# Layer 1's output projection as seven half-size products, with positions as rows

## The chip, the cores and the metric

The kernel runs on one core of one Trainium2 chip. The metric is the time of one execution on the device, in microseconds (us). The kernel before takes 930.77 us, the median of 3 runs (930.66 to 931.35).

## The reference, cut to what matters

Two layers work on x, 512 positions by 1024 features: an mLSTM mixer, then a gated linear attention (GLA) mixer. Each ends with an output projection, an RMSNorm over the features and a residual. What the change touches is the end of layer 1:

```python
def gla_mixer(h, w_in, w_gate_up, b_gate, norm_w, w_out):
    ...
    on = o * lax.rsqrt(jnp.mean(o * o, axis=-1, keepdims=True) + NORM_EPS)
    y = on.reshape(B, T, D_INNER) * _f32(norm_w) * jax.nn.silu(z)
    return jnp.einsum('bte,ed->btd', y, _f32(w_out))
...
    x = x + rms_norm(out, post_norm_w[i]).astype(x.dtype)
```

y is 512 x 2048, w_out is 2048 x 1024.

## The kernel before, in words

Everything is float32 in and out. To multiply at the fast format of TensorE (PE), each operand is split into a high part (a cast on ScalarE, ACT, L133) and a low part (a subtraction on VectorE, DVE, L134), and a product is three matmuls: high x high, high x low, low x high.

Activations lie with features on the partitions and positions in the free axis. The program is a list of jobs in the order of PE (`job`, `run_jobs`, from L137). A job that needs weights names a chunk, 128 x 1024; chunks are loaded by SyncE's queue (SP) into three buffers (`raw`), split into four pairs (`whi`, `wlo`), and are split LA = 3 chunks ahead of the job that runs. PE, ACT and DVE keep the order of the program; GpSimd (POOL) and SP are ordered by the scheduler. `later(k, fn)` puts off work on other engines by k jobs, `steps` spreads it over jobs.

Layer 1's head h has four jobs `gv`, attention (`g_att`, L1071), four jobs `gz`, and `g_y` (L1082), which multiplies y's blocks by their norm and splits them (`y_split`). The output projection (`out_stage(1, ...)`, L1120) then takes the weights as stationary operand and y as moving operand, half of the sequence at a time, 256 columns: 16 blocks of y's features x 8 blocks of output x 2 halves x 3 = 768 matmuls. A chunk serves 24 or 48 of them. The sum of squares over features crosses partitions, so it goes through PE as well (`rstd_of`, `ssq`). `residual` (L769) reads layer 0's result x1 back from memory (stored by `x1_done`, L829), scales and adds. The output is written transposed, features by positions, and the host turns it.

The lines that matter in the stage:

```python
            proj(ps, chunk, yhi[r], ylo[r], c == 0, c == 1, sl)
            if c == 1:
                ...
                nc.scalar.mul(pair(OUT["o", half, n // 2])[:, n % 2, :], ps, col(PV_POST + KD * layer + n))
```

Of the kernel before, what the change touches and what calls it, by code (L numbers as in the profile page):

```python
# [16 lines left out]
P = 128  # L17
# [5 lines left out]
NH = 4  # L23
# [69 lines left out]
def tile_mlstm_gla(ctx, tc, xT, pvec, cst, wg, wgv, w_min, w_qk, w_v, w_mout,  # L93
                   w_gqk, w_gr, w_gu, w_gv, w_gz, w_gout, lvl_masks, outT):
# [22 lines left out]
    def mm(out, lhsT, rhs, start, stop):  # L117
        nc.tensor.matmul(out, lhsT=lhsT, rhs=rhs, start=start, stop=stop)  # L118
# [51 lines left out]
    def run_jobs():  # L170
        srcs = [x for j in jobs for x in j[1]]
        raws, ready, used = [], [], 0
        for fn, ss, n, b, la in jobs:
            used += len(ss)
            while len(ready) < min(used + la, len(srcs)):
                while len(raws) < min(len(ready) + 3, len(srcs)):
                    raws.append(load_raw(srcs[len(raws)][0]))
                i = len(ready)
                ready.append(split_chunk(raws[i], srcs[i][1]))
# [6 lines left out]
            for _ in range(n):  # L186
# [9 lines left out]
    ring = lambda ap: (ap, "ring")  # L196
    keep = lambda ap: (ap, "keep")

# [82 lines left out]
    # The first projections take x * w; their rstd follows when it is known.  # L281
# [46 lines left out]
    # the part of the gates that comes from v, by products with rows of weights  # L328
# [200 lines left out]
    # gates: rows (head, block) of log i and log f, their decays and running maximum  # L529
# [206 lines left out]
    def out_full(layer, n, mid=None):  # L736
        """Rows 128 n of out^T from the first half of its inputs, for all of the sequence."""
# [7 lines left out]
        job(run, ring((w_mout, w_gout)[layer][2 * n]))  # L745

    def out_job(layer, n, c, half, after=None):
        """A half of the sequence of rows 128 n of out^T, from the half c of its inputs."""
        sl = HALF[half]

        def run(chunk):
# [17 lines left out]
        job(run, ring((w_mout, w_gout)[layer][2 * n + c]))  # L769

    def residual(half, src, done, last=False):
        """Steps of out = x + rms_norm(out), in place, for a half of the sequence."""
# [14 lines left out]
        def add(k):  # L787
# [3 lines left out]
            if k > 1:  # L791
                done(k - 2, pair(o(k - 2)), half)
            if 1 <= k <= KP:
                eng = nc.gpsimd if last and k == 2 else nc.vector
                eng.tensor_add(o(k - 1), o(k - 1), xr[k - 1])  # L795
# [4 lines left out]
    def out_stage(layer, early, after_half, done=0, ahead=0):  # L800
        for n in range(done, NF):
            out_full(layer, n, early if n == done and not layer else None)
            if n == done and layer:
                job(early, n=0)
        for n in range(NF, NF + ahead):
            out_job(layer, n, 0, 0)
        for half in range(2):
            for n in range(KD):
                if n >= NF + ahead * (half == 0):
                    out_job(layer, n, 0, half)  # L810
                out_job(layer, n, 1, half, after_half if (n, half) == (0, 1) else None)

    for h in range(NH):
        job(lambda h=h: (m_num(h), m_scale(h), m_skip(h)), n=0)
        if h < NH - 1:
# [16 lines left out]
    def x1_done(kp, x1, half):  # L832
# [12 lines left out]
        nc.sync.dma_start(x1_d[half, kp], x1)  # L845

    def after_half0():
        rstd, add = residual(0, x_rows, x1_done)
# [10 lines left out]
    # projections take x1 * w; their rstd follows  # L859
# [120 lines left out]
    def kept_a(w, j, kind, la=LA):  # L980
# [4 lines left out]
        job(run, (w_gqk[w, j], kind), n=2, la=la)  # L985
# [97 lines left out]
    def g_y(h, vt):  # L1083
# [46 lines left out]
    def early1():  # L1130
        g_rstd(NH - 1)
        steps.extend([lambda v=v: (g_y(NH - 1, v), g_y(NH - 1, v + 1)) for v in (0, 2)])

    def x_done(k, x, half):
        nc.sync.dma_start(outT[2 * k * P:2 * (k + 1) * P, HALF[half]].rearrange("(a p) t -> p a t", p=P), x)

    x1_rows = lambda k, half: pair(x1_d[half, k])

    def after_half1():
        rstd, add = residual(0, x1_rows, x_done)  # L1140
        steps.append(rstd)
        for k in range(KP + 2):
            steps.extend([lambda k=k: add(k), lambda: None])
# [7 lines left out]
def _host(inputs):  # L1151
# [46 lines left out]
    out["w_gout"] = outc(a["g_w_out"].reshape(E, D))  # L1198
    lm = np.zeros((8, P, P), np.int32)
    for i, half in enumerate([64, 32, 16, 8, 4, 2, 1]):  # L1200
# [7 lines left out]
        "w_gqk", "w_gr", "w_gu", "w_gv", "w_gz", "w_gout", "lvl_masks"]  # L1208
# [18 lines left out]
```

## Time and profile before

| | |
|---|---|
| median of 3 runs | 930.77 us (930.66 to 931.35) |
| span of the profiled execution, first to last instruction | 928.9 us |
| the profiled execution's own time | not listed apart; the median lies 1.9 us above its span |
| PE busy | 916.0 us, 99% |
| DVE busy | 617.2 us, 66% |
| ACT busy | 516.4 us, 56% |
| POOL busy | 150.8 us, 16% |
| mean granted clock of TensorE | 0.997 |
| bytes moved | 114.06 MB, mean 123 GB/s |

Busy time is the time in which an engine had an instruction under way; PE's matmuls overlap, so a busy PE is not a PE at its peak. Idle time of an engine matters where another one waits for it. The stage that the change replaces begins at 824.1 us and ends with the span.

### The profile page before, as it was taken

The page shows a single profiled execution, that of the slowest core. Times are in us where ns is not written, and L with a number is a line of the kernel's source. Part 1 is how long each engine was busy: PE and PEld are TensorE (multiplying, and loading weights), DVE is VectorE, ACT ScalarE, POOL GpSimd, SP SyncE. Part 2 cuts the span into 40 slices and gives each one's busy share as a digit, 9 for nine tenths or more (in the row PEclk, how much of TensorE's full clock was granted, in tenths as well). Part 3 has the DMA queues.
Part 4 walks back from the last instruction along what each step waited for, and adds up shares of the span by engine and source line. Part 5 has one row for each costly group of instructions (what it writes and reads, how often), then busy time and mean ns, then how long its engine had stood idle before and what let it go on. Part 6 is the DMA issues. An engine that isn't in the chain of part 4 may idle for free. (4 is left out here: it accounts for less than half of the span.)

```text
span 928.9 us, 13051 instructions
## 1 busy us (share of the span) xinstructions
PE 916.0 (99%) x5030; PEld 787.8 (85%) x5030; DVE 617.2 (66%) x863; ACT 516.4 (56%) x855; POOL 150.8 (16%) x111
## 2 busy tenths in 40 slices
PE   9999999999999999999999999999999999999995
PEld 6887878878877888899999987778888888899995
DVE  5999897787795668787668666642446454565563
ACT  6856676655754657775666454553335353545451
POOL 0022563163240045233002100000000000000000
PEclk9999999999999999999999999999999999999998
DMA  8334353442431323332777322122312222124573
GB/s 313 118 111 147 114 167 128 134 150 91 146 126 46 93 66 114 114 114 94 219 247 237 133 72 87 68 69 93 91 68 73 87 91 91 58 62 152 184 227 114
DMA packets 41669, 114.06 MB, mean 123 GB/s; under 512 B 4545, under 2 KB 9025, under 8 KB 41601
## 3 DMA queue, kind: packets, MB, share of 16 engines
q1 hardware_dynamic: 41312, 112.95, 37.6%
q8 instruction: 41, 0.67, 0.3%
q14 instruction: 28, 0.22, 0.1%
q10 hardware_dynamic: 288, 0.22, 0.1%
HBM read 104.76 MB, written 8.39 MB: 122 GB/s over the span
## 5 line engine op out<-in xcount | busy, mean ns | idle before, releaser
L134 DVE TENSOR_TENSOR wlo<-raw,whi 128x1024 fp32r<-128x1024 f32 (+1 forms) x159 | 202.8, 1280 | 138.3 <-ACT whi L133 137.4
L133 ACT CAST whi<-raw 128x1024 fp32r<-128x1024 f32 (+1 forms) x159 | 164.2, 1037 | 99.2 <-PE gv L118 37.7
L118 PE MATMUL op<-yhi,whi 128*128 128x256 f32 x512 | 146.5, 286 | 0.0
L118 PE MATMUL op<-yhi,wlo 128*128 128x256 f32 x512 | 144.9, 283 | 0.4 <-DVE wlo L134 0.4
L118 PE MATMUL op<-ylo,whi 128*128 128x256 f32 x512 | 145.3, 284 | 0.0
L341 POOL TENSOR_TENSOR vp<-V,wv 128x512 f32<-128x512 f32 x56 | 88.5, 1603 | 177.3 <-ACT V L429 109.1
L118 PEld LDWEIGHTS op<-ylo,whi 128*128 128x128 f32 x512 | 98.2, 192 | 1.3 <-issue 0.7
L118 PEld LDWEIGHTS op<-yhi,whi 128*128 128x128 f32 x512 | 98.2, 192 | 0.8 <-issue 0.7
L118 PEld LDWEIGHTS op<-yhi,wlo 128*128 128x128 f32 x512 | 98.2, 192 | 0.6 <-DVE wlo L134 0.6
L344 DVE SCALAR_TENSOR_TENSOR vp<-V,wv 128x512 f32<-128x512 f32 x72 | 68.0, 985 | 0.0
L118 PE MATMUL gz<-g2h,whi 128*128 128x512 f32 x128 | 51.6, 403 | 0.3 <-PEq L1067 0.3
L118 PE MATMUL gz<-g2h,wlo 128*128 128x512 f32 x128 | 49.9, 390 | 0.0
L118 PE MATMUL gz<-g2l,whi 128*128 128x512 f32 x128 | 49.9, 389 | 0.0
L118 PE MATMUL qk<-chi,whi 128*128 128x512 f32 x128 | 49.8, 389 | 0.0
L118 PE MATMUL qk<-chi,wlo 128*128 128x512 f32 x128 | 49.8, 389 | 0.0
L118 PE MATMUL qk<-clo,whi 128*128 128x512 f32 x128 | 49.8, 389 | 0.0
L118 PE MATMUL gv<-whi,g2h 128*128 128x512 f32 x128 | 49.8, 389 | 0.0
L118 PE MATMUL gv<-wlo,g2h 128*128 128x512 f32 x128 | 49.8, 389 | 0.0
L118 PE MATMUL gv<-whi,g2l 128*128 128x512 f32 x128 | 49.8, 389 | 0.0
L795 POOL TENSOR_TENSOR o<-o,xr 128x512 f32<-128x512 f32 x1 | 1.5, 1491 | 293.6 <-DVE o L790 293.6
L118 PE MATMUL z<-hhi,whi 128*128 128x512 f32 x112 | 44.2, 394 | 0.0
L118 PE MATMUL z<-hlo,whi 128*128 128x512 f32 x112 | 43.6, 390 | 0.0
(240 smaller groups left out, 2219.5 us busy)
## 6 DMA issues: line engine op xcount, KB each, us to landing
raw<-in_w_min SPq DMA_DIRECT2D x30, 512.0 KB, 3.7
raw<-in_w_mout SPq DMA_DIRECT2D x29, 512.0 KB, 4.2
raw<-in_w_gout SPq DMA_DIRECT2D x29, 512.0 KB, 3.5
wv<-in_wgv SPq DMA_DIRECT2D x32, 256.0 KB, 3.5
raw<-in_w_qk SPq DMA_DIRECT2D x16, 512.0 KB, 3.5
raw<-in_w_gqk SPq DMA_DIRECT2D x16, 512.0 KB, 3.7
raw<-in_w_gz SPq DMA_DIRECT2D x16, 512.0 KB, 3.4
raw<-in_w_gv SPq DMA_DIRECT2D x16, 512.0 KB, 3.5
```

Source lines behind the costliest of these rows:

```text
L118: nc.tensor.matmul(out, lhsT=lhsT, rhs=rhs, start=start, stop=stop)
L133: nc.scalar.copy(hi, src)
L134: nc.vector.tensor_sub(lo, src, hi.bitcast(F32))
L341: nc.gpsimd.tensor_mul(j, V[h][i], w)
L344: nc.vector.scalar_tensor_tensor(j, V[h][i], 1.0, w, op0=ALU.mult, op1=ALU.mult, accum_out=o)
L795: eng.tensor_add(o(k - 1), o(k - 1), xr[k - 1])
```

## The change

The two products of 2 x 2 blocks (y: halves of the positions by halves of its 2048 features; weights: halves of the features by halves of the outputs) are made by seven products of blocks instead of eight. y's block is now the stationary operand (128 positions at a time), the weights move, 512 wide, and positions are the output's rows. Each product is 4 chunks x 2 blocks of 128 positions x 2 feature blocks x 3 = 48 matmuls of 512 columns. P1 to P7 name the products; a job takes one chunk c of one, 12 matmuls: P1 0, P5 0, P1 1, P5 1, and so on, then P2, P3, P6, P7 mixed, and P4 at the end, 24 matmuls for each block of positions.

The sums and differences of weight blocks are formed chunk by chunk on POOL (`p5`, `p2`, `p7`, 16 instructions of 128 x 1024), those of y's blocks on POOL for k below 4 and for heads 0 and 1, and on DVE for the others (`combine`). y's blocks and their combinations are split as operands 1 to 4. With positions as rows, the norm's sum is taken by ACT along the free axis, and the post-norm weight, now along the free axis, comes as a row (`pw`). x1 is therefore needed with positions as rows: `turn` transposes it on PE in layer 0's output stage, 4 transposes for each of 8 tiles. A chunk may have its own buffers (`home`, tiles of the pool t5), is formed up to FLA chunks before it is split and loaded up to HLA chunks ahead. The output is written as it is wanted.

```diff
+FLA = 2
+HLA = 3
+NRAW = 3
...
-        job(run, ring((w_mout, w_gout)[layer][2 * n + c]))
+        job(run, ring(w_mout[2 * n + c]))
...
-        nc.sync.dma_start(x1_d[half, kp], x1)
+        x1 = pair(x1)
+
+        def turn():
+            ps, xn = psum("xt"), t2("xn")
+            for j in range(2):
+                for i in range(2):
+                    nc.tensor.transpose(ps[:, (2 * j + i) * P:(2 * j + i + 1) * P],
+                                        x1[:, i, j * P:(j + 1) * P], ident)
+            nc.scalar.copy(xn, ps)
+            nc.sync.dma_start(x1_d[2 * half:2 * half + 2, :, kp * 256:(kp + 1) * 256].rearrange("j p c -> p j c"),
+                              xn.rearrange("p (j c) -> p j c", j=2))
+
+        later(8 if half == 0 else 4, turn)
...
         nc.vector.tensor_mul(y, y, st["rs", h])
-        if vt:
-            y_split(h, [vt - 1])
-        if vt == 3:
-            y_split(h, [3])
+        if h < 2:
+            Y[0, n] = y
+            nc.gpsimd.tensor_sub(y[:, HALF[1]], y[:, HALF[1]], y[:, HALF[0]])
+        else:
+            Y[1, n - 8] = y
...
+        if h == NH - 1:
+            job(lambda: [operand("2", k, Y[1, k]) for k in range(4)], n=0)
+            job(lambda: [combine(k, nc.gpsimd) for k in range(4)], n=0)
         job(lambda h=h: g_att(h))
...
+                if h == 2:
+                    job(lambda i=i: [operand("1", k, Y[0, k]) for k in range((0, 2, 5)[i - 1], (2, 5, 8)[i - 1])], n=0)
...
+    def operand(name, k, src):
+
+        OPS[name, k] = t2("yhi", F32R), t2("ylo", F32R)
+        split(*OPS[name, k], src)
+
+    def combine(k, eng):
+
+        y1, y2 = Y[0, k], Y[1, k]
+        a, b = HALF
+        eng.tensor_sub(y1[:, b], y2[:, b], y1[:, b])
+        eng.tensor_sub(y1[:, a], y1[:, b], y1[:, a])
+        eng.tensor_sub(y2[:, a], y2[:, a], y1[:, b])
...
+    def p5(c):
+        def f(a21, a22):
+            nc.gpsimd.tensor_add(a21, a21, a22)
+            sm[c] = a21
+            return a21
+
+        def to_s2():
+            sub(sm[c], sm[c], raw11[c])
+
+        return source([(w_gout[1, 0, c], lambda: t5("sm")[:, 0:1024]), (w_gout[1, 1, c], None)], form=f,
+                      after=to_s2, free=(1, 0))
...
+        def to_s4():
+            sub(raw12[c], raw12[c], sm[c])
...
+    def p7(c):
+        def f(a22):
+            sub(sm[c], a22, sm[c])
+            raw22[c] = a22
+            return sm[c]
+
+        def to_p4():
+            last[c] = split_chunk(raw22[c], "t2")
...
+    for c in range(4):
+        prod_job("P1", c)
+        prod_job("P5", c)
+        if c == 1:
+            job(lambda: (g_rstd(NH - 1), steps.extend(
+                [lambda: tail_y(0), lambda: tail_y(2), lambda: None, lambda: None]
+                + [lambda k=k: (combine(k, nc.vector), combine(k + 1, nc.vector)) for k in (4, 6)]
+                + [lambda k=k: (operand("3", k, Y[0, k]), operand("3", k + 1, Y[0, k + 1])) for k in range(0, 8, 2)]
+                + [lambda c=c: operand4(c) for c in range(4)])), n=0)
...
+    for name, c in (("P2", 0), ("P2", 1), ("P3", 0), ("P2", 2), ("P3", 1), ("P2", 3), ("P3", 2),
+                    ("P6", 0), ("P6", 1), ("P6", 2), ("P6", 3), ("P3", 3), ("P7", 0), ("P7", 1), ("P7", 2)):
+        prod_job(name, c)
+    job(lambda: [load_res(r) for r in (2, 3)], n=0)
+    prod_job("P7", 3)
+    job(lambda: [load_res(r) for r in (0, 1)], n=0)
+
+    def last_row(r):
+        part_sum(r, 1, bank["a", r])
+        part_scale(r, 1, bank["a", r], nc.vector)
+        row_done(r)
+
+    job(lambda: product("P4", "a", last, 0), n=2)
+    job(lambda: (product("P4", "a", last, 1), last_row(0), last_row(1)), n=13)
```

How the change moves instructions is shown at three places. First DVE, from the last head's gz jobs to the evacuation of its attention (`g_att(3)`); pt are y's blocks, ylo their low parts, wlo a chunk's low part. Before:

```order
L1097 TENSOR_TENSOR gz_8444<-gz,rs_238 128x512
L1086 TENSOR_TENSOR pt_8225<-pt_8225,rs 128x512
L134 TENSOR_TENSOR ylo_8449<-pt_8224,yhi_8448 128x512
L1086 TENSOR_TENSOR pt_8226<-pt_8226,rs 128x512
L134 TENSOR_TENSOR ylo_8454<-pt_8225,yhi_8453 128x512
L134 TENSOR_TENSOR ylo_8458<-pt_8226,yhi_8457 128x512
L1079 SCALAR_TENSOR_TENSOR pt_8461<-o,pv,gz_8325 128x512
```

And now:

```order
L1144 TENSOR_TENSOR gz_8505<-gz,rs_238 128x512
L1132 TENSOR_TENSOR pt_8263<-pt_8263,rs_8369 128x512
L1132 TENSOR_TENSOR pt_8264<-pt_8264,rs_8369 128x512
L138 TENSOR_TENSOR ylo_8511<-pt1_7892,yhi_8510 128x512
L138 TENSOR_TENSOR ylo_8515<-pt2_7893,yhi_8514 128x512
L138 TENSOR_TENSOR ylo_8519<-pt3_7894,yhi_8518 128x512
L138 TENSOR_TENSOR ylo_8523<-pt0_8261,yhi_8522 128x512
L138 TENSOR_TENSOR ylo_8527<-pt1_8262,yhi_8526 128x512
L138 TENSOR_TENSOR ylo_8531<-pt2_8263,yhi_8530 128x512
L138 TENSOR_TENSOR ylo_8535<-pt3_8264,yhi_8534 128x512
L1125 SCALAR_TENSOR_TENSOR pt0_8550<-o_8554,pv_80,gz12_8364 128x512
```

Seven ylo splits stand between the last gz and the first product of g_att(3), where three stood.

Second POOL, around the stage's start; sm and raw are weight chunks, a is the chunk of P1, pt are y's blocks. Before, POOL's list from layer 1's scores to the end is:

```order
L975 AFFINE_SELECT GA_6132<-GA_6132 128x128 x4
L1066 TENSOR_LOAD wide
L1067 COMPARE_AND_BRANCH
L1067 UNCONDITIONAL_BRANCH x2
L795 TENSOR_TENSOR o<-o,xr 128x512
L1223 UNCONDITIONAL_BRANCH
```

Now, from the first weight sum on:

```order
L1241 TENSOR_TENSOR sm<-sm,raw 128x1024 x2
L1200 TENSOR_TENSOR pt_7525<-pt_8261,pt_7525 128x256
L1201 TENSOR_TENSOR pt_7525<-pt_7525 128x256
L1246 TENSOR_TENSOR sm<-sm,a_8183 128x1024
L1200 TENSOR_TENSOR pt_7526<-pt_8262,pt_7526 128x256
L1201 TENSOR_TENSOR pt_7526<-pt_7526 128x256
L1241 TENSOR_TENSOR sm<-sm,raw 128x1024
```

After these come nine more instructions on y's blocks and twelve more on weight chunks of 128 x 1024, then six that scale parts of the output.

Third DVE within the stage, before, where a chunk's split and a sum of squares alternate:

```order
L134 TENSOR_TENSOR wlo<-raw,whi 128x1024 x2
L257 TENSOR_TENSOR sq<-sq 128x256
L134 TENSOR_TENSOR wlo<-raw,whi 128x1024 x2
L257 TENSOR_TENSOR sq<-sq 128x256
L134 TENSOR_TENSOR wlo<-raw,whi 128x1024
```

And now, from P2 2's split on (L1200 to L1202 are `combine`):

```order
L1200 TENSOR_TENSOR pt_7893<-pt_8552,pt_7893 128x256
L1201 TENSOR_TENSOR pt_7893<-pt_7893 128x256
L1202 TENSOR_TENSOR pt_8552<-pt_8552,pt_7893 128x256
L1200 TENSOR_TENSOR pt_7894<-pt_8553,pt_7894 128x256
L1201 TENSOR_TENSOR pt_7894<-pt_7894 128x256
L1202 TENSOR_TENSOR pt_8553<-pt_8553,pt_7894 128x256
L138 TENSOR_TENSOR wlo<-raw,whi 128x1024
L138 TENSOR_TENSOR ylo<-pt_7525,yhi 128x512
L138 TENSOR_TENSOR ylo<-pt_7526,yhi 128x512
L138 TENSOR_TENSOR wlo<-raw,whi 128x1024
```

Between two splits there now stand six combinations or two splits of y's blocks, and a chunk is 12 matmuls, not 24 or 48.

## Rows read from the trace of the kernel before

**Rows 1.** Page, part 1: busy us (share of the span) xinstructions.

```profile
PE 916.0 (99%) x5030; PEld 787.8 (85%) x5030; DVE 617.2 (66%) x863; ACT 516.4 (56%) x855; POOL 150.8 (16%) x111
```

**Rows 2.** Chain of waits in order of time: start us, us, what.

```profile
764.40 21.76 PE gv L118 x96
...
824.10 5.80 PE op L118 x48
829.90 0.86 PE ssq L118 x2
830.76 51.82 PE op L118 x432
882.58 0.43 PE ssq L118 x2
883.01 34.54 PE op L118 x288
917.55 0.43 PE ssq L118 x2
...
918.03 0.71 PE ssq L118 x2
```

**Rows 3.** Tile rc (ns min/median/max, starts), and PE's timeline at 536.5 us.

```profile
L915 PE MATMUL rc<-cs,rs x4: 271/272/273, 536.6 to 536.9; 128*128 128x128 f32 x4
...
536.55 0.60 PE L915 MATMUL rc<-cs,rs 128*128 128x128 f32 x4
```

**Rows 4.** Timelines of POOL and DVE, 921 us on: start, us, what [idle before].

```profile
921.25 1.49 POOL L795 TENSOR_TENSOR o<-o,xr 128x512 f32<-128x512 f32 x1 [293.60 <-DVE o L790]
...
923.81 1.28 DVE L795 TENSOR_TENSOR o<-o,xr 128x512 f32<-128x512 f32 x2
```

**Rows 5.** Groups by form, whole run (first two), 824 on (last): busy, mean ns | idle.

```profile
L133 ACT CAST whi<-raw 128x1024 fp32r<-128x1024 f32 x155 | 161.8, 1048 | 97.9 <-PE gv L118 37.7 <-PE gqk L118 29.2 <-PE op L118 13.7
...
L257 DVE TENSOR_TENSOR sq<-sq 128x256 f32<-128x256 f32 x27 | 11.3, 420 | 10.4 <-ACT sq L254 10.4
...
L134 DVE TENSOR_TENSOR wlo<-raw,whi 128x1024 fp32r<-128x1024 f32 x26 | 31.9, 1225 | 28.2 <-ACT whi L133 28.2
```

**Rows 6.** DVE's timeline at 837 us, POOL at rest.

```profile
837.50 1.23 DVE L134 TENSOR_TENSOR wlo<-raw,whi 128x1024 fp32r<-128x1024 f32 x1 [1.18 <-ACT whi L133]
838.65 0.68 DVE L1086 TENSOR_TENSOR pt<-pt,rs 128x512 f32<-128x512 f32 x1
839.25 0.68 DVE L134 TENSOR_TENSOR ylo<-pt,yhi 128x512 fp32r<-128x512 f32 x1
```

**Rows 7.** DVE's timeline at 126 and 228 us, POOL at work throughout.

```profile
126.13 1.28 DVE L134 TENSOR_TENSOR qkl<-qk,qkh 128x512 fp32r<-128x512 f32 x2
...
228.68 1.78 DVE L344 SCALAR_TENSOR_TENSOR vp<-V,wv 128x512 f32<-128x512 f32 x1
...
230.39 1.76 DVE L344 SCALAR_TENSOR_TENSOR vp<-V,wv 128x512 f32<-128x512 f32 x1
...
232.08 2.30 DVE L134 TENSOR_TENSOR wlo<-raw,whi 128x1024 fp32r<-128x1024 f32 x1
234.31 1.78 DVE L344 SCALAR_TENSOR_TENSOR vp<-V,wv 128x512 f32<-128x512 f32 x1
```

**Rows 8.** POOL's timeline at 327 us, one instruction with gaps on both sides.

```profile
327.17 1.29 POOL L646 TENSOR_TENSOR sq<-sq 128x512 f32<-128x512 f32 x1 [60.78 <-ACT sq L644]
```

**Rows 9.** Timelines of DVE and ACT around the end of g_att(3).

```profile
821.01 1.40 DVE L1079 SCALAR_TENSOR_TENSOR pt<-o,pv,gz 128x512 f32<-128x512 f32 x2
...
826.99 1.04 ACT L133 CAST whi<-raw 128x1024 fp32r<-128x1024 f32 x1
...
828.05 1.23 DVE L134 TENSOR_TENSOR wlo<-raw,whi 128x1024 fp32r<-128x1024 f32 x1 [0.24 <-ACT whi L133]
```

**Rows 10.** Page, part 6: DMA issues, KB each, median us to landing.

```profile
raw<-in_w_gout SPq DMA_DIRECT2D x29, 512.0 KB, 3.5
```

**Rows 11.** Windows: PE, PEld, DVE, ACT, POOL busy, PEclk, DMA share, GB/s.

```profile
923.00:924.00 1.00, 0.00 (x0) 0.00 (x0) 1.00 (x3) 0.00 (x0) 0.00 (x0) 0.65 0.66 222
```

More of the change, by code (lines that the diff above doesn't have):

```diff
@@ L115, in psum, with mm @@
         return pp.tile([P, T], F32, tag="ps", bufs=8, name=name)
-    def mm(out, lhsT, rhs, start, stop):
-        nc.tensor.matmul(out, lhsT=lhsT, rhs=rhs, start=start, stop=stop)
+    def mm(out, lhsT, rhs, start, stop, more=False):
+        nc.tensor.matmul(out, lhsT=lhsT, rhs=rhs, start=start, stop=stop, skip_group_check=more)
     HALF = [slice(0, T // 2), slice(T // 2, T)]
@@ L185, in run_jobs @@
                 x[1]()
-            for _ in range(n):
+            for _ in range(steps_n):
                 if steps:
@@ L194, in run_jobs, with source @@
         jobs.clear()
-    ring = lambda ap: (ap, "ring")
-    keep = lambda ap: (ap, "keep")
+    def source(loads, kind="ring", form=None, after=None, free=(0, 1)):
+        return dict(loads=loads, kind=kind, form=form, after=after, free=free)
+    ring = lambda ap: source([(ap, None)])
     use(SILU)
@@ L734, in pair, with out_full @@
         return t.rearrange("p (a t) -> p a t", a=2)
[L736 removed]
+    def out_full(n, mid=None):
         def run(chunk):
@@ L743, in run, with out_job @@
                     mid()
-        job(run, ring((w_mout, w_gout)[layer][2 * n]))
-    def out_job(layer, n, c, half, after=None):
+        job(run, ring(w_mout[2 * n]))
+    def out_job(n, c, half, after=None):
         sl = HALF[half]
@@ L791, in add, with out_stage @@
             if k > 1:
-                done(k - 2, pair(o(k - 2)), half)
+                x1_done(k - 2, pair(o(k - 2)), half)
             if 1 <= k <= KP:
-                eng = nc.gpsimd if last and k == 2 else nc.vector
-                eng.tensor_add(o(k - 1), o(k - 1), xr[k - 1])
+                nc.vector.tensor_add(o(k - 1), o(k - 1), xr[k - 1])
                 load(k + 1)
         return rstd, add
-    def out_stage(layer, early, after_half, done=0, ahead=0):
+    def out_stage(early, after_half, done=0, ahead=0):
         for n in range(done, NF):
-            out_full(layer, n, early if n == done and not layer else None)
-            if n == done and layer:
-                job(early, n=0)
+            out_full(n, early if n == done else None)
         for n in range(NF, NF + ahead):
-            out_job(layer, n, 0, 0)
+            out_job(n, 0, 0)
         for half in range(2):
@@ L1128, in tile_mlstm_gla @@
                 job(lambda h=h, i=i: (g_y(h, i - 1), g_y(h, 3) if i == 3 else None))
[L1130 to L1143, printed above, removed]
@@ new lines, in operand4, with block @@
+    def operand4(c):
+        OPS["4", c] = t2("yhi", F32R), t2("ylo", F32R)
+        for i in range(2):
+            split(*(z[:, HALF[i]] for z in OPS["4", c]), Y[1, 2 * c + i][:, HALF[0]])
+    def block(name, k):
+        what, half = {"P1": ("1", 0), "P5": ("1", 1), "P2": ("2", 0), "P3": ("2", 1),
+                      "P7": ("3", 0), "P6": ("3", 1), "P4": ("4", k % 2)}[name]
+        return [z[:, HALF[half]] for z in OPS[what, k // 2 if what == "4" else k]]
+    bank, sums, parts = {}, {}, {}
@@ new lines, in product @@
+    def product(name, to, chunks, tb, c0=0):
+        if (to, tb) not in bank:
+            bank[to, tb] = psum("op")
+        ps = bank[to, tb]
+        for c, (whi, wlo) in enumerate(chunks):
+            for i in range(2):
+                k = 2 * (c0 + c) + i
+                yh, yl = (z[:, tb * P:(tb + 1) * P] for z in block(name, k))
+                more = name in ("P6", "P7", "P4", "P3")
+                mm(ps, yh, whi[i], k == 0 and not more, False, more)
+                mm(ps, yh, wlo[i], False, False, more)
+                mm(ps, yl, whi[i], False, k == 7, more)
@@ new lines, in tile_mlstm_gla, with p1, f @@
+    sm, raw11, raw12, raw22, last = ([None] * 4 for _ in range(5))
+    sub = nc.gpsimd.tensor_sub
+    def p1(c):
+        def f(a11):
+            raw11[c] = a11
+            return a11
+        return source([(w_gout[0, 0, c], lambda: t5("a11")[:, 0:1024])], form=f, free=(0, 0))
+    def p5(c):
[7 more added lines that the diff above has]
+                      after=to_s2, free=(1, 0))
@@ new lines, in tile_mlstm_gla, with prod_job, run @@
+    SRC = {"P1": p1, "P5": p5, "P2": p2, "P7": p7, "P3": lambda c: source([], form=lambda: raw12[c]),
+           "P6": lambda c: source([], form=lambda: sm[c], free=(0, 0))}
+    TO = {"P1": "a", "P6": "a", "P7": "a", "P4": "a", "P5": "c", "P3": "c", "P2": "d"}
+    def prod_job(name, c, n=1, la=LA):
+        def run(chunk):
+            for tb in range(2):
+                product(name, TO[name], [chunk], tb, c)
+            if c == 3:
+                if name in ("P1", "P5", "P6", "P7"):
+                    AFTER[name]()
+                else:
+                    later(8 if name == "P2" else 2, AFTER[name])
+        job(run, SRC[name](c), n=n, la=la)
@@ new lines, in keep_copy, with load_res, part_sum @@
+    def keep_copy(name, to):
+        for tb in range(2):
+            sums[name, tb] = t2(name)
+            nc.scalar.copy(sums[name, tb], bank[to, tb])
+    ssq = cp.tile([P, 8], F32, name="ssq")
+    rso = cp.tile([P, 4], F32, name="rso")
+    res = {}
+    def load_res(r):
+        for m in range(2):
+            res[r, m] = t2("xr")
+            nc.sync.dma_start(res[r, m], x1_d[r, :, m * T:(m + 1) * T])
+    def part_sum(r, m, src):
+        junk = t2("sq")
+        nc.scalar.activation(junk, src, AF.Square, accum_out=ssq[:, 2 * r + m:2 * r + m + 1])
@@ new lines, in part_scale, with out_part, row_done @@
+    def part_scale(r, m, src, eng):
+        if (r, m) not in parts:
+            parts[r, m] = t2("o")
+        eng.tensor_mul(parts[r, m], src, st["pw"][:, m * T:(m + 1) * T])
+    def out_part(r, m, to, name, tb):
+        parts[r, m] = t2("o")
+        nc.vector.tensor_add(parts[r, m], bank[to, tb], sums[name, tb])
+        part_sum(r, m, parts[r, m])
+        part_scale(r, m, parts[r, m], nc.gpsimd)
+    def row_done(r):
+        c = rso[:, r:r + 1]
+        use(LNEXP)
+        nc.vector.tensor_add(c, ssq[:, 2 * r:2 * r + 1], ssq[:, 2 * r + 1:2 * r + 2])
+        nc.scalar.activation(c, c, AF.Ln, bias=epst, scale=1.0 / D)
+        nc.scalar.activation(c, c, AF.Exp, scale=-0.5)
+        for m in (0, 1):
+            o = parts[r, m]
+            nc.vector.scalar_tensor_tensor(o, o, c, res[r, m], op0=ALU.mult, op1=ALU.add)
+            nc.sync.dma_start(out[r * P:(r + 1) * P, m * T:(m + 1) * T], o)
@@ new lines, in after_p6, with after_p7, after_p3 @@
+    def after_p6():
+        keep_copy("u2", "a")
+    def after_p7():
+        for tb in range(2):
+            out_part(2 + tb, 1, "a", "e5", tb)
+        row_done(2)
+        row_done(3)
+    def after_p3():
+        for tb in range(2):
+            out_part(2 + tb, 0, "c", "u2", tb)
+    AFTER = {"P1": lambda: keep_copy("e1", "a"), "P5": lambda: keep_copy("e5", "c"), "P6": after_p6,
+             "P2": lambda: [out_part(tb, 0, "d", "e1", tb) for tb in range(2)], "P7": after_p7, "P3": after_p3}
@@ new lines, in tail_y @@
+    def tail_y(v):
+        g_y(NH - 1, v)
+        g_y(NH - 1, v + 1)
+        for k in (4 + v, 5 + v):
+            operand("2", k, Y[1, k])
+    for c in range(4):
[7 more added lines that the diff above has]
+                + [lambda c=c: operand4(c) for c in range(4)])), n=0)
```

91 lines of the change are left out of this document (62 added, 29 removed).

## The prediction

> **What bounds the kernel now.** I read the page's engine shares first: TensorE (PE) is busy 99% of the span, no other engine over 66% [rows 1]. That says where the limit is, not what the last stage costs, so I read the chain of waits in order of time next. From 824.10 to 917.55 us it is layer 1's output projection, matmul after matmul, with no wait between them [rows 2]. 48, 432 and 288 matmuls take 5.80 + 51.82 + 34.54 = 92.16 us, 120.0 ns for each 256 columns. The same view has 96 matmuls of 512 columns (gv) in 21.76 us, 226.7 ns each [rows 2]. So PE sets the time, and whatever replaces this stage either runs at PE's pace or makes PE wait.
>
> **PE, counted.** 768 matmuls of 256 columns go, 7 products x 48 = 336 of 512 come: 336 x 0.2267 = 76.2 us, **-16.0 us**. An eighth of the columns is Strassen's, the rest is the wider form (240 against 226.7 ns per 512 columns). The Trainium skill (TensorE: Matmul & The Clock Gate, Back-to-back issue gap) gives N/2.4 + 2.5 ns, 109 and 216 ns here, by which the gain would be an estimated 11 us; the rows are slower in both forms and decide. The sum of squares over features leaves PE: -0.43 us [rows 2]. Added are 32 transposes of x1 in layer 0's output stage. Four such transposes took 0.60 us from first start to last end with 0.27 for one, so 0.11 each [rows 3]: **+3.5 us**, since PE has no idle time there to hide them. Their 8 copies on ACT and the stores lie beside PE; without that cover they would cost 8 x 0.6 = 5 us, which I count at nothing.
>
> **The tail.** Before, the last matmul of op ended at 917.55, and then came the sum matmuls, Ln, Exp, seven passes on VectorE (DVE) and one on GpSimd (POOL) until 925.09, then 3.8 us for the last store [rows 2, 4]. After, behind the last matmul: one square with its sum on ACT (about 0.8), add, Ln, Exp on one column (about 0.7 with their hand-overs), two passes on DVE (1.3), the same 3.8: 6.6 to 7.0 against 11.3. **-4.3 us.** Row groups 2 and 3 and the rows of y's blocks finish under P4, 48 matmuls or 10.9 us.
>
> Without new waits the span would be 928.9 - 16.0 - 0.4 + 3.5 - 4.3 = 911.7. The median of the runs lies 1.9 us above the profiled span, so 913.6 us.
>
> **The waits.** This is the term that decides. A chunk was 48 matmuls, 5.8 us; now it is 12, 2.72 us, and still split only three chunks ahead, since its tile is the one that PE leaves three jobs before (the casts already wait for PE [rows 5]). Meanwhile DVE and POOL get more work. DVE's price by starts in a row with POOL at rest: 1.15 us for a 1024-wide split, 0.60 for a 512-wide operation [rows 6], about 0.34 for 256 (0.42 in all [rows 5], less the overlap).
>
> POOL now works beside them, 293 us of rest before [rows 4] becoming 26 operations. With both at work DVE's starts lie 1.71 us apart (512) and 2.23 (1024), where alone they are 0.60 and 1.15 [rows 6, 7]. Each DVE operation with two SBUF inputs lets one POOL operation go first and pays 1.10 us; one with a PSUM input pays nothing (126.13: 2 in 1.28 us) [rows 7]. So the two **take turns**, and their times add. The Trainium skill (SBUF — State Buffer, Who interferes with whom) has the same exclusive turn, held for the whole instruction. By that rule a 512-wide POOL operation would cost DVE its full 1.29 us instead of the 1.10 seen, and the result would be about 5 us worse (14 x 0.35).
>
> POOL's combinations of weights are 1024 wide, and no row has such a one. Bounds: 1.10 us, if width does not matter, and 2.5, twice the 1.29 of a lone one [rows 8]. I take 2.18, twice 1.10, as 1.10 us for 512 columns is what two reads in turn would look like; 0.55 for 256.
>
> Now the budget, from gz14's start, 14.5 us before P1 (809.6 in the old trace), to the split of the last chunk, P7 3. By DVE's order: 23 splits x 1.15 + 39 operations of 512 x 0.60 + 20 of 256 x 0.34 = 56.7 us. POOL: 14 of 1024 x 2.18 + 12 of 256 x 0.55 = 37.1 us. Together **93.8 us**. PE needs 14.5 + 23 x 2.72 + 0.86 = 77.9 us to come to P7 3. So PE waits at least 15.9 us. Behind it DVE has two klo splits and five sums to do (4.5 us) before P4 may write bank a, P7 3 covers 2.7 of it: 17.7 in all. That is the floor, with no gap in the turns: 913.6 + 17.7 = 931.3 us.
>
> There are gaps. I followed the orders operation by operation with these prices (zero is P1's start). POOL's combine and its two weight operations fall among 12 ylo splits; DVE, which reached g_att(3)'s products 3.1 us before zero [rows 9], reaches them at about +6. From there the chain is the old one: product, square on ACT, sum, in turn, and behind it the cast and split of the next chunk, 8.3 us from 821.01 to 829.28 [rows 9], plus POOL's add for P5 3 in between. So P5 1, due at 8.2, has its high part at about 14 and its low part at 15.4: **the first and longest wait, 6 to 7 us**. P2 0 to P3 0 wait about 5 us more behind y's last head (g_y, ylo) and POOL's S2 and S4, the jobs from P3 1 to P6 2 some 1 to 2 us each while combine, operands 3 and 4 and POOL's S4 and P7 forms take turns, P7 3's bank 1.8. P4 starts at 87.5 instead of 66.1: **+21.4 us**. 913.6 + 21.4 = **935.0 us**.
>
> Loads: 28 reads of 512 KB in place of 32, 3.5 us to land [rows 10]. S2's tile for P5 2 is asked for only when a11 is released, at about -9.5, and lands near -5.7, before its turn; for P5 3 when g_att(3) ends, landing near +4.5. P7's last two come behind P3 3's and P7 0's splits and land in time. I cost them at nothing; each us late would add as much.
>
> **Rivals.**
> - *PE keeps its pace* (the other side). If POOL's 1024-wide operations hold the port for 1.10 us, the budget falls by 14 x 1.08 = 15.1 us to 78.7, about PE's 77.9, and 21.4 - 15.1 gives 919.9 us; with no wait at all 913.6. The place is the port between -14.5 and +80; the point from which it decides is a POOL price of about 1.9 us, at which the sum meets the old time (0.3 x 14 = 4.2 us off). For it: of the old stage's 26 splits all idle time ahead, 28.2 us, was ended by a cast, not by the port [rows 5], so some turns may fall into such gaps. Against: the turns in [rows 7] have no gap. 0.25.
> - *Packed turns.* Both engines always have something ready: the floor, 931.3 us. For it: three chunks of lead. Against: in-order queues, and POOL's adds wait for loads and for splits. 0.18.
> - *The clock falls.* The granted clock, 1.00 over the stage, was 0.65 in the us from 923 [rows 11], on the way from 2.4 to 1.2 GHz, with no matmul since 918.7 [rows 2]. The wait at P5 1 is longer than that. Then P5 1 and what follows go at half pace, 2.7 us for each chunk, and g_rstd(3) comes later by as much; a part hides under the port: 938 to 941 us. 0.15.
> - *The change does less than it says.* The program's list has 336 op matmuls of 512 and none of 256 for layer 1: excluded.
>
> **How the numbers follow.** The forecast by the walk, 935.0 (932.6 to 938), has 0.42. A difference under 0.2%, 1.9 us, is what runs of this kernel cannot tell from none. Faster than 928.9 is the first rival, 0.25; within 928.9 to 932.6 the packed turns, 0.18; slower the walk and the clock, 0.57. The range leaves out a tenth on each side: 922 takes in most of the first rival, 941 the clock and the dearer POOL price. The likeliest cases' own range is 931 to 938.
>
> **What would show it.** Right: op matmuls of 512 columns, 0.227 us apart where they run; 32 transposes at 0.11; PE idle first at the fourth chunk, P5 1, ended by ACT's or DVE's split of sm, 5 us or more; in all some 20 us of idle PE between P1 and P4; DVE splits of 1.23 us stretched to over 3 us beside POOL; a tail of about 7 us. Wrong: PE without gaps in the stage, or POOL's 128x1024 operations near 1.3 us long, gives the first rival; PE waiting on loads (DMA) gives a cause that I costed at nothing; waits in layer 0 at the transposes likewise.

## The result, and the profile after

The changed kernel takes 937.61 us, the median of 4 runs (936.81 to 937.85), against 930.78 us before: ratio 1.0072, interval 1.0058 to 1.0086. It is slower, inside the range, 2.6 us above the forecast of 935.0. The profiled span is 935.1 us; the median lies 2.5 us above it.

The page's engine shares answer to [rows 1]:

```profile
PE 907.2 (97%) x4624; PEld 761.7 (81%) x4624; DVE 653.5 (70%) x886; ACT 523.2 (56%) x876; POOL 224.3 (24%) x152
```

PE is busy for 9 us less and the program is 6 us longer, so PE now waits. PE's view of waits, from 795 us on, names for whom (us in total, times, longest):

```profile
PE op L122 <- ACT whi L137: 8.9, 2, 7.1
PE op L122 <- DVE wlo L138: 8.6, 9, 1.5
PE op L122 <- DVE o L1314: 1.0, 1, 1.0
```

Every wait but the last is for a chunk's split. PE's timeline shows where; the number in brackets is the idle time before:

```profile
827.52 0.44 PE L122 MATMUL op<-whi,yhi 128*128 128x512 f32 x1
...
835.52 0.39 PE L122 MATMUL op<-whi,ylo 128*128 128x512 f32 x1
843.05 0.80 PE L122 MATMUL op<-whi,yhi 128*128 128x512 f32 x1 [7.14 <-ACT whi L137]
844.31 0.79 PE L122 MATMUL op<-wlo,yhi 128*128 128x512 f32 x1 [0.47 <-DVE wlo L138]
844.90 0.63 PE L122 MATMUL op<-whi,ylo 128*128 128x512 f32 x1
845.33 0.63 PE L122 MATMUL op<-whi,yhi 128*128 128x512 f32 x1
...
847.65 0.39 PE L122 MATMUL op<-wlo,yhi 128*128 128x512 f32 x1
847.88 0.39 PE L122 MATMUL op<-whi,ylo 128*128 128x512 f32 x1
...
864.55 0.50 PE L122 MATMUL op<-whi,yhi 128*128 128x512 f32 x1 [1.80 <-ACT whi L137]
...
884.00 0.50 PE L122 MATMUL op<-wlo,yhi 128*128 128x512 f32 x1 [1.52 <-DVE wlo L138]
```

The stage begins at 827.52 (before: 824.10 [rows 2]). After 36 matmuls comes the first wait, at the fourth chunk, P5 1: 7.5 us from start to start, then 1.3 more for the low part. Behind it matmuls follow each other every 0.43 us, which is 1.2 GHz (granted clock 0.52 from 843 to 847 us), and from 847 on every 0.23, 2.4 GHz again (1.00 from 848). Of the 335 distances between starts of op matmuls 305 are 0.228 us on average; twelve long ones hold 21.0 us of waits (the view above has 18.5, since a matmul's span reaches over the start of the next), the six at half pace or on the way back 1.3 us, and the second matmul behind a wait comes 0.11 late nine times, 1.0 us.

The chain of waits ends with the tail:

```profile
917.30 11.19 PE op L122 x48
...
928.51 0.70 ACT sq L1304 x2
...
930.71 1.30 DVEq L1456
```

The last matmul ends at 928.49, the span at 935.1: 6.6 us, where it was 11.35 [rows 2, 4]. So the 6.2 us between the spans are +3.4 (later start of the stage), +7.5 (the stage itself, 101.0 for 93.45) and -4.7 (tail). The transposes of x1 account for the first:

```profile
L885 PE MATMUL xt<-cs,o x32: 272/272/273, 502.2 to 522.2; 128*128 128x128 f32 x32
```

How DVE and POOL met is seen best where POOL has one sum alone among DVE's splits. POOL's timeline, then DVE's:

```profile
879.52 2.73 POOL L1257 TENSOR_TENSOR raw<-raw,sm 128x1024 f32<-128x1024 f32 x1 [6.41 <-DVE wlo L138]
```

```profile
879.30 3.50 DVE L138 TENSOR_TENSOR ylo<-pt,yhi 128x512 fp32r<-128x512 f32 x2
882.73 1.21 DVE L138 TENSOR_TENSOR wlo<-raw,whi 128x1024 fp32r<-128x1024 f32 x1
883.86 1.28 DVE L138 TENSOR_TENSOR ylo<-pt,yhi 128x512 fp32r<-128x512 f32 x2
```

Two splits of 512 take 1.28 us alone and 3.50 beside POOL's sum: one sum of 1024 takes 2.22 us out of DVE's time. The forecast had 2.18.

### The profile page after: what moved, and what is told of

Its sections match the earlier page's. It is cut to its first block, busy times and chain, and to the rows that moved or that the text cites. A ratio compares the mean times of both kernels' runs of the same rounds, so it can differ in the third digit from the quotient of the medians.

```text
span 935.1 us, 12315 instructions
## 1 busy us (share of the span) xinstructions
PE 907.2 (97%) x4624; PEld 761.7 (81%) x4624; DVE 653.5 (70%) x886; ACT 523.2 (56%) x876; POOL 224.3 (24%) x152
## 5 line engine op out<-in xcount | busy, mean ns | idle before, releaser
L138 DVE TENSOR_TENSOR wlo<-raw,whi 128x1024 fp32r<-128x1024 f32 (+1 forms) x138 | 180.4, 1313 | 117.5 <-ACT whi L137 116.1
L137 ACT CAST whi<-raw 128x1024 fp32r<-128x1024 f32 (+1 forms) x138 | 142.6, 1038 | 96.4 <-PE gv L122 37.7
L122 PE MATMUL op<-yhi,whi 128*128 128x256 f32 x256 | 73.4, 287 | 0.0
L122 PE MATMUL op<-yhi,wlo 128*128 128x256 f32 x256 | 72.5, 283 | 0.4 <-DVE wlo L138 0.4
L122 PE MATMUL op<-ylo,whi 128*128 128x256 f32 x256 | 72.8, 284 | 0.0
L122 PEld LDWEIGHTS op<-ylo,whi 128*128 128x128 f32 x256 | 49.1, 192 | 1.1 <-DVE ylo L138 0.6
L122 PEld LDWEIGHTS op<-yhi,wlo 128*128 128x128 f32 x256 | 49.1, 192 | 0.6 <-DVE wlo L138 0.6
L122 PEld LDWEIGHTS op<-yhi,whi 128*128 128x128 f32 x256 | 49.1, 192 | 0.5 <-issue 0.5
L122 PE MATMUL op<-whi,yhi 128*128 128x512 f32 x96 | 38.7, 403 | 8.9 <-ACT whi L137 8.9
L122 PE MATMUL op<-wlo,yhi 128*128 128x512 f32 x96 | 39.0, 406 | 8.6 <-DVE wlo L138 8.6
```

Of the source, the lines that this page charges most:

```text
L137: nc.scalar.copy(hi, src)
L138: nc.vector.tensor_sub(lo, src, hi.bitcast(F32))
```

## The experiments

My theory was the one on record: DVE and POOL take turns at what both read SBUF through, so POOL's sums make DVE's splits late, and PE waits for those. Rivals: DVE's own list is too long, POOL itself is late, the clock's fall, or the form with positions as rows.

**1. The sums on DVE.**

```diff
-            nc.gpsimd.tensor_add(a21, a21, a22)
+            nc.vector.tensor_add(a21, a21, a22)
...
-    sub = nc.gpsimd.tensor_sub
+    sub = nc.vector.tensor_sub
...
-            job(lambda: [combine(k, nc.gpsimd) for k in range(4)], n=0)
+            job(lambda: [combine(k, nc.vector) for k in range(4)], n=0)
```

> The 16 sums of weight blocks and the combinations for k below 4 go from POOL to DVE; the work is the same. Theory (DVE and POOL take turns, so their times add): on DVE a 1024-wide sum costs 1.15 us where POOL's took 2.18 out of DVE's time, so the budget of 93.8 us becomes 56.7 + 14 x 1.15 + 12 x 0.34 = 76.9 us, about PE's 77.9. Most waits go: the one at P5 1 falls from 7.5 to about 3 us, 3 to 5 us are left elsewhere, 920 to 925 us. Rival (POOL works beside DVE at no cost, and DVE's own list is the limit): DVE gets 20 us more to do, its budget goes from 56.7 to 76.9 and the time stays or rises, 935 to 945 us.

Measured: 933.53 us, ratio 1.0028 [1.0018, 1.0038]. Below the change though DVE got all of POOL's sums of weights and its combinations, which speaks for the turns, but 8 us above the range that I expected. P5 1 waited 4.1 us for its high part and 1.6 for its low part, where I had expected about 3 in all. What I had missed stands in DVE's view of waits from 825 us on:

```profile
DVE sm L1263 <- DMA raw<-in_w_gout: 6.4, 2, 3.4
```

P7's sums (L1263), formed two chunks ahead, now stood in DVE's queue before the splits that free the raw buffer they wait for. POOL had kept that wait off DVE.

**2. Without the sums.** The 16 sums of weights are left out.

```diff
-            nc.gpsimd.tensor_add(a21, a21, a22)
...
-            sub(sm[c], sm[c], raw11[c])
...
-            sub(raw12[c], raw12[c], sm[c])
...
-            sub(sm[c], a22, sm[c])
```

> POOL's 16 sums of weight blocks are left out, so the products are of other blocks; loads, splits, matmuls and the combinations of y stay. Theory (turns): budget 56.7 + 12 x 0.55 = 63.3 us against PE's 77.9; POOL's two sums before g_att(3) go too, 4.4 us, so P5 1 waits some 2 us instead of 7.5 and the clock stays up; 915 to 919 us. Rival (DVE's order and the lead of three chunks make the waits): P5 1 still waits 5 us or more, over 928 us.

Measured: 916.8 us, ratio 0.9852 [0.9835, 0.9868], inside the theory's 915 to 919. The rival needed over 928. PE's waits are down to

```profile
PE op L122 <- ACT whi L137: 1.4, 1, 1.4
PE op L122 <- DVE wlo L138: 0.8, 1, 0.8
```

**3. POOL writes but does not read.**

```diff
-            nc.gpsimd.tensor_add(a21, a21, a22)
+            nc.gpsimd.memset(a21, 0.5)
...
-            sub(raw12[c], raw12[c], sm[c])
+            nc.gpsimd.memset(raw12[c], 0.5)
```

and so for the other two.

> Each of POOL's 16 sums of weight blocks becomes a fill of the same tile with a constant, at the same place and with the same waits on other engines except those for what it read; the products are of constants where sums stood. Theory (it is POOL's reads that take turns with DVE's): DVE's splits beside a fill take 1.2 to 1.3 us, not 2 to 3, and the time is near that of the run without sums, 915 to 921 us. Rival A (any POOL instruction holds the turn): DVE's splits stay stretched, 928 us or more. Rival B (it is POOL's lateness, not the turns): also above 928 if a fill takes as long as a sum, with DVE idle before splits.

Measured: 917.36 us, ratio 0.9855 [0.9839, 0.9871]. As the theory has it; but a fill took only 0.96 us, so POOL was earlier as well. That is mended in the next run.

**4. Three fills for each sum**, as long as a sum.

```diff
-            sub(sm[c], sm[c], raw11[c])
+            nc.gpsimd.memset(sm[c], 0.25)
+            nc.gpsimd.memset(sm[c], 0.25)
+            nc.gpsimd.memset(sm[c], 0.25)
```

> Each of POOL's 16 sums becomes three fills of the same tile, some 2.9 us in all, as long as a sum took, so POOL is as late as with sums but reads nothing. Theory (reads take turns, writes do not): as with one fill, 916 to 920 us. Rival (POOL's lateness makes the waits): 925 us or more, with ACT's casts of sm waiting for POOL.

Measured: 915.5 us, ratio 0.9838 [0.9822, 0.9853]. POOL's timeline, and DVE's beside it:

```profile
837.51 0.96 POOL L1248 MEMSET sm<- 128x1024 f32 x1 [3.32 <-DVE wlo L138]
838.53 0.96 POOL L1249 MEMSET sm<- 128x1024 f32 x1
839.54 0.95 POOL L1250 MEMSET sm<- 128x1024 f32 x1
```

```profile
837.37 1.22 DVE L138 TENSOR_TENSOR wlo<-a,whi 128x1024 fp32r<-128x1024 f32 x1
838.51 1.22 DVE L138 TENSOR_TENSOR wlo<-sm,whi 128x1024 fp32r<-128x1024 f32 x1
```

DVE's splits run at 1.22 us with POOL busy all the while. That POOL's work takes long is out as the cause, and so is any cost of POOL that does not read: it is POOL's reads. One thing else goes with the reads: a fill does not wait for the load of what a sum would read. In the change POOL stood 1.3 us before P5 2's sum, whose load was issued at 819.8 us, and P7 2's sum came late behind its own load, 1.6 of PE's 21.0 us. This part was not separated; it is small beside the 20 us. The Trainium skill (SBUF — State Buffer, Who interferes with whom) has a DVE instruction with two SBUF inputs contend with a GpSimd instruction that reads SBUF and not with one that only writes it. For the one that only writes the rows above agree, for the one that reads the rows at 879 us in the section on the result.

**5. Rows, without Strassen.** One part alone: 16 chunks, each with four blocks of positions, the last four chunks kept and taken row block by row block.

```diff
-    for c in range(4):
-        prod_job("P1", c)
-        prod_job("P5", c)
...
+    for f in range(8):
+        row_job(0, f)
...
+    for f in range(4):
+        row_job(1, f)
...
+    for r in range(4):
+        job(lambda r=r: last_row(r), n=13)
```

> One part alone: positions as rows, y stationary and weights moving 512 wide, but the plain product, 16 chunks of 24 matmuls (the last four row block by row block), no sums of blocks and nothing on POOL in the stage. 384 matmuls x 0.2267 = 87.05 us for 92.16: -5.1; sum of squares -0.4; transposes +3.5; tail -4.3. A chunk is 5.4 us of PE and one split, so no waits. 930.8 - 6.3 = 924.5 us, 922.5 to 926. Rival (waits come from the rows form itself: its last head's y comes late, or its row sums at the end cost more): 928 us or more, with PE idle in the stage.

Measured: 924.34 us, ratio 0.9933 [0.9916, 0.9949]. In this run the two halves' indices of the weights were exchanged. With each chunk from its place:

> As the run before of the rows form with eight products, with each chunk of weights from its place (that run had the two indices of the halves exchanged, same sizes and same number of loads). The time does not hang on which chunk is loaded: 924.3 us, 923.5 to 925. Rival: none but a load that lands late, seen as PE waiting for DMA.

Measured: 924.84 us, ratio 0.9936 [0.9923, 0.9950]. The chain of this run:

```profile
828.12 10.95 PE op L122 x48
839.06 0.86 PE ssq L122 x2
839.92 76.19 PE op L122 x336
...
916.13 0.70 ACT sq L1197 x2
...
918.32 1.30 DVEq L1337
```

384 matmuls without a wait, 87.1 us, then a tail of 7.1 us. So the rows form alone is worth 6 us, and Strassen's eighth, as the change has it, takes 12.8 us back: 10.9 us of matmuls saved, 21.0 of waits and 2.3 of slow and late matmuls paid.

**6. Sums on DVE, each formed when its chunk is split**, as 1 else, to take the loads' wait away.

```diff
-FLA = 2
+FLA = 0
```

> All sums on DVE as in the first run, and a chunk is formed only when it is split (FLA 0 in place of 2). In the first run DVE's sums for P7 2 and P7 3 stood in its queue ahead of the splits that free the raw buffer they wait for (6.4 us of DVE idle, ended by raw loads). Theory: these 6 to 8 us go, P5 1's wait of 4 us and the clock's fall behind it stay: 925 to 928 us. Rival (the turns were not the cause, DVE's list is too long as such): no better than 932.

Measured: 936.25 us, ratio 1.0061 [1.0045, 1.0076]. Missed: the number is the rival's, 932 or more. And with the combinations of y for k below 4 moved behind g_att(3):

```diff
-                [lambda: tail_y(0), lambda: tail_y(2), lambda: None, lambda: None]
+                [lambda: tail_y(0), lambda: tail_y(2)]
+                + [lambda k=k: (combine(k, nc.vector), combine(k + 1, nc.vector)) for k in (0, 2)]
```

> As the run with sums on DVE and late forming, and the 12 combinations of y for k below 4 move from before g_att(3) to the two empty steps at P1 3 and P5 3. Theory: DVE reaches g_att(3)'s products 4 us earlier, P5 1 does not wait, or under 1 us, the clock stays at 1.00; what is left are waits of 1 us or less where DVE's 76.9 us of work stand against PE's 77.9: 917 to 922 us, below the rows form with eight products. Rival (the wait only moves to P2 0 to P3 0 by the same amount): 924 to 928.

Measured: 935.79 us, ratio 1.0054 [1.0040, 1.0067]. Missed too, and DVE's timeline says why:

```profile
836.48 1.22 DVE L1240 TENSOR_TENSOR sm<-sm,raw 128x1024 f32<-128x1024 f32 x1
838.81 1.23 DVE L138 TENSOR_TENSOR wlo<-sm,whi 128x1024 fp32r<-128x1024 f32 x1 [1.11 <-ACT whi L137]
```

Sum, cast and split of one chunk follow each other on DVE, ACT and DVE, and DVE, which keeps its order, rests 1.1 us while ACT casts: 8.7 us in all. So the rival's number has another cause than the length of DVE's list, as the next run shows with the same list: I had put the sums in the wrong place.

**7. Sums on DVE, formed one chunk ahead.**

```diff
-FLA = 2
+FLA = 1
...
-        return source([(w_gout[1, 1, c], None)], form=f, after=to_p4)
+        home = (lambda: t5("a22")[:, 0:1024]) if c < 2 else None
+        return source([(w_gout[1, 1, c], home)], form=f, after=to_p4, free=(0, 1 if home is None else 0))
```

> As the run with sums on DVE, late forming and moved combinations, but a chunk is formed one chunk ahead of its split (FLA 1), and P7 0 and P7 1 load A22 into the tiles that the chunks a11 have left. Theory: with forming at the split, DVE stood idle 8.7 us behind ACT's casts of what it had just formed, ACT's copies of bank a stood behind those casts (4.1 us of PE), and P7's loads came late; with one chunk between sum and split all of it goes: 919 to 924 us. Rival (DVE's list of 77 us against PE's 78 leaves no room for any order): 928 us or more.

Measured: 925.96 us, ratio 0.9951 [0.9937, 0.9964]: 11.7 us below the change with the same sums made, and no turns with POOL; 2 us above my range. DVE's idle time behind casts falls from 8.7 to 0.7 us. Two things differ from the run before, the distance of one chunk and P7's tiles, and three from experiment 1; they were not tried apart. PE's waits and two stretches of the windows (PE, PEld, DVE, ACT, POOL busy, PEclk, DMA share, GB/s):

```profile
PE op L122 <- DVE wlo L138: 6.1, 7, 1.6
PE op L122 <- ACT whi L137: 2.1, 2, 1.3
```

```profile
865.00:875.00 10.00, 7.64 (x32) 5.40 (x31) 9.79 (x18) 7.91 (x12) 0.00 (x0) 1.00 0.16 53
...
885.00:895.00 10.00, 10.00 (x45) 8.09 (x44) 10.00 (x15) 5.77 (x10) 0.00 (x0) 1.00 0.08 28
```

DVE is busy 9.8 to 10 of 10 us in these stretches, and 68.3 of 70 from 835 to 905, where PE's waits for splits lie. So what is left of them goes by DVE's list; experiment 10 takes work off that list.

**8. The change, with only POOL's combinations moved**, as in 6.

> The change as it is, with POOL's sums; only POOL's 12 combinations of y for k below 4 move from before g_att(3) to the two empty steps at P1 3 and P5 3. Theory (a budget of 93.8 us of port against PE's 77.9): the wait at P5 1 falls from 7.5 to about 3 us and the clock stays up, but the same port time is paid later in the stage, floor 931.3: 931 to 935 us. Rival (the first wait and the clock's fall are the loss): 926 to 929.

Measured: 936.81 us, ratio 1.0068 [1.0053, 1.0084]. It tells nothing: POOL's order is the scheduler's, and its list came out the same, instruction for instruction, as did the first wait (7.0 us). The edit moved a line of the program, not the work.

**9. The clock by itself.** 29 matmuls that nobody reads go into the first wait.

```diff
+    def fill():
+        ps = psum("fill")
+        yh = OPS["1", 0][0]
+        for _ in range(29):
+            mm(ps, yh[:, 0:P], yh, True, True)
...
         prod_job("P1", c)
+        if c == 1:
+            job(fill, n=0)
```

> The change as it is, with 29 matmuls of 512 columns that nobody reads put on PE between P1 1 and P5 1, 6.6 us, inside the wait of 7.5 us. They measure what the clock's fall costs. Theory (the clock falls because PE rests): the granted clock stays at 1.00 from 835 to 855 us, P5 1 and P1 2 run at 0.227 us a matmul, and the end comes 2 to 3 us earlier: 934.5 to 936 us. Rival (the port sets the pace there, so the clock costs nothing): 937 to 938.

Measured: 936.63 us, ratio 1.0066 [1.0052, 1.0080], 1.0 us below the change, with intervals that overlap. The windows, of the change and then of this run, show that the clock stayed up:

```profile
843.00:848.00 5.00, 4.49 (x12) 3.28 (x13) 4.97 (x3) 4.12 (x4) 3.30 (x1) 0.61 0.01 3
```

```profile
843.00:848.00 5.00, 4.24 (x16) 2.92 (x17) 5.00 (x3) 4.10 (x5) 3.31 (x1) 1.00 0.00 0
```

DVE is busy 4.97 and 5.00 of 5 us in both. What PE gains there it loses at the next chunks: PE now waits at 859.36 and the clock falls at 864 instead. PE's timeline of this run:

```profile
864.36 0.80 PE L122 MATMUL op<-whi,yhi 128*128 128x512 f32 x1 [2.21 <-ACT whi L137]
...
866.65 0.63 PE L122 MATMUL op<-whi,yhi 128*128 128x512 f32 x1
```

The fall was moved, then, not taken away, and it is longer: 2.7 us of slower matmuls for 1.3. Even so DVE's split for P3 2, which PE waits for in both, starts at 882.60 us, and in the change at 882.80, with a stage that began 0.16 later. Neither fall moves that point: the slow matmuls took the place of waits, since at P3 0, P3 1 and P2 3, where the change waits 2.3 us in all, this run does not wait. The clock's fall costs 1 us or less here; I had expected 2 to 3. A run without any fall was not made.

**10. Sums on DVE, y's work earlier.** As 7; operand 1 is made beside gv(3), operand 2's first blocks and two combinations beside gz13 to gz15.

```diff
                 gv_job(h + 1, c)
+                if h == 2:
+                    job(lambda c=c: [operand("1", k, Y[0, k]) for k in (2 * c, 2 * c + 1)], n=0)
```

> As the run with sums on DVE formed one chunk ahead, but work on y goes ahead of the stage: operand 1 (eight splits of y's blocks) is made beside head 3's gv jobs, where DVE is busy 3 to 6 of 10 us, operand 2's first four blocks beside gz13 to gz15, and two of the combinations for k below 4 there as well. Theory (with all sums on DVE, DVE's list is the limit: 9.3 of 10 us busy from 835 to 905, 9.2 us of PE waits): 5 splits x 0.6 + 6 operations of 256 x 0.34 = 5 us leave DVE's full stretch, and the waits fall by about as much: 919 to 922.5 us, below the rows form with eight products. Rival (the earlier operands take tiles that others wait for, or delay gv's splits): PE waits before 827 us, 926 us or more.

Measured: 924.53 us, ratio 0.9933 [0.9920, 0.9947]: 1.4 us better than 7 and 2 above my range. The waits for splits and bank a fell from 9.2 to 5.1 us, as thought, but a part came back ahead of the stage:

```profile
804.66 1.12 PE L122 MATMUL ssq<-sq,cs 128*128 128x512 f32 x2 [1.08 <-DVE sq L297]
```

One of the early splits of y stood 4.6 us in DVE's queue for a tile that PE's attention still read, and g_att(2)'s sum of squares behind it came 1.1 us late. Behind P2 1's wait eight matmuls also ran at about half pace, 1.7 us, which they did not in 7 (last section). 4.1 us less, 1.1 and 1.7 more make 1.3 less, near the 1.4 measured; that each of them is worth what it shows was not tried. This version and the rows form (924.84) beat both kernels by the same amount; the rows form is the simpler one.

## Why the prediction was right, and where it was not

**PE, counted: right.** 336 matmuls run 0.228 us apart where they run. The Trainium skill (TensorE: Matmul & The Clock Gate, Back-to-back issue gap) has 0.216 for 512 columns as the gap of a matmul by itself, which no stretch of this stage shows. **Transposes: right**, +3.5 forecast, +3.4 measured. **Tail: right**, -4.3 forecast, -4.7 measured.

**The price of POOL's sum: right.** 2.18 us forecast from a 512-wide row, 2.22 measured, less than the 2.73 that POOL's row lasts. [rows 7] pointed at what experiments 2 to 4 show by taking the sums, and then only their reads, away: 20 us and more hang on those reads. The rival "PE keeps its pace" needed a price under 1.9 us and falls with it.

**The waits: 21.4 us forecast, 21.0 measured, but with three errors that cancel.** That the sum came out so close is luck; that POOL's reads make the waits is not. The first error is in the budget: "39 operations of 512". The groups by form of DVE, 813.2 to 911.8, the same stretch, count 24 + 7 + 6 + 3 and 6 more with one PSUM input, 46. The first three kinds:

```profile
L138 DVE TENSOR_TENSOR ylo<-pt,yhi 128x512 fp32r<-128x512 f32 x24 | 27.9, 1203 | 1.4 <-ACT yhi L137 1.2
...
L1132 DVE TENSOR_TENSOR pt<-pt,rs 128x512 f32<-128x512 f32 x7 | 10.5, 1540 | 0.0
L138 DVE TENSOR_TENSOR klo<-raw,khi 128x512 fp32r<-128x512 f32 x6 | 3.9, 683 | 0.0
```

Seven too few, 4.2 us. The second is POOL's part. Without POOL, in experiment 7, the same ylo splits take 686 ns on average:

```profile
L138 DVE TENSOR_TENSOR ylo<-pt,yhi 128x512 fp32r<-128x512 f32 x24 | 15.2, 686 | 1.4 <-ACT yhi L137 1.2
```

So 24 of them were stretched by 24 x (1.203 - 0.686) = 12.4 us; with the other forms, reckoned the same way, POOL took 28 us of DVE's time and not 37.1, nine less, since a part of its work fell into DVE's gaps. These gaps are the third error. The windows of the change:

```profile
813.20:911.90 98.70, 81.12 (x351) 63.95 (x350) 89.02 (x89) 51.10 (x78) 53.42 (x26) 0.97 0.25 83
```

DVE is idle for 9.7 of 98.7 us, before splits and sums that wait for ACT; the walk had 21.4 - 17.7 = 3.7 us of gaps. The floor, 931.3 us, rested on 37.1 and was no floor: with 60.9 us of DVE's own work and 28 of POOL's the same sum gives 913.6 + 11.0 + 1.8 = 926.4 us. The 9.7 us of gaps make up most of the rest: 936.1 against 937.6.

**Where the waits fall: right in kind.** P5 1 was forecast first and longest at 6 to 7 us; it was 8.3 with its low part. The path was the one forecast: seven ylo splits, stretched beside POOL's combine to 1.23 us each but one, held DVE off g_att(3)'s products until 7.0 us after P1's start (forecast about 6), and ACT's cast of P5 1 stood behind the squares of those products. DVE's timeline:

```profile
827.04 7.56 DVE L138 TENSOR_TENSOR ylo<-pt,yhi 128x512 fp32r<-128x512 f32 x7
834.52 1.40 DVE L1125 SCALAR_TENSOR_TENSOR pt<-o,pv,gz 128x512 f32<-128x512 f32 x2
```

P2 0 to P3 0 had 3.8 in place of 5, P3 1 to P6 2 had 6.2 in all, and the last bank 1.1 instead of 1.8. P7 2 waited 1.6 us, which the prediction did not have: it cost P7's loads at nothing, but this one was issued at 899.0 us, and POOL's sum for it began at 902.7. The loads themselves were miscounted, which changed nothing: 20 chunks of w_out are read in the change (12 to `raw`, 4 to `a`, 4 to `sm`), not 28.

**The clock, a rival at 0.15, happened and hardly counted.** It fell, as that rival said, behind P5 1's wait, 1.3 us of slower matmuls. Its price of 3 to 6 us was wrong: with the clock held up at that place the kernel gains 1.0 us at most, because PE waits for DVE again at P3 2 in any case (experiment 9).

The 2.6 us between forecast and result are, as the trace has them, the slower matmuls (1.3) and the late second matmuls (1.0) in the stage, and 0.6 because the median lies 2.5 and not 1.9 us above the span, less 0.4 of tail; 0.4 of waits less and 0.4 for 0.228 in place of 0.2267 us a matmul cancel. By experiment 9 the 1.3 would mostly have been waits had the clock stayed up.

## What to carry to other kernels

A saving on the busiest engine is worth what the others can feed it: before halving a chunk's matmuls, add up what DVE and POOL must do for each chunk, and count a POOL instruction that reads SBUF beside two-input DVE work as DVE time, at up to twice DVE's price (2.22 us against 1.15 for 1024 columns here; about three quarters of that over the stage, where gaps took the rest). Moving such work to DVE, idle POOL or not, gained 11.7 us, but of the runs made here only where each sum stood one chunk ahead of its split (and P7's tiles and y's combinations had moved as well): not two, where its load blocked the queue, and not none, where the cast did. Try the parts of a large change alone: the plain half of this one was the gain.

## What the runs showed of the hardware that I had not expected

- POOL's fills of 128 x 1024 take 0.96 us, and DVE's splits beside them 1.22 us, as alone. A POOL sum of the same size takes 2.34 to 3.3 us, once 4.6, and stretches them: the split of P5 2's sum took 3.41 us.
- PE's clock does not follow the length of the last wait alone. In experiments 7 and 10 the same pair of waits, 1.27 and 0.76 us, stands before the same matmuls; in the first they go on every 0.23 us, 2.4 GHz, in the second every 0.43, 1.2 GHz (granted clock from 855 to 865 us 1.00 and 0.83):

```profile
857.62 0.50 PE L122 MATMUL op<-wlo,yhi 128*128 128x512 f32 x1 [0.75 <-DVE wlo L138]
857.96 0.40 PE L122 MATMUL op<-whi,ylo 128*128 128x512 f32 x1
858.20 0.39 PE L122 MATMUL op<-whi,yhi 128*128 128x512 f32 x1
```

```profile
859.34 0.56 PE L122 MATMUL op<-wlo,yhi 128*128 128x512 f32 x1 [0.76 <-DVE wlo L138]
859.69 0.63 PE L122 MATMUL op<-whi,ylo 128*128 128x512 f32 x1
860.12 0.63 PE L122 MATMUL op<-whi,yhi 128*128 128x512 f32 x1
```

What differs before them was not tried.
